# An hgrn2, LRU and attention stack on one core: y transposed right behind its gates, and the even layer's gate products in other PSUM banks

## The chip, the cores and the metric

The program runs on one core of one Trainium2 chip. A core has a matrix engine (PE; its weight loads are listed apart as PEld), a vector engine (DVE), a scalar engine (ACT), a general engine (POOL), and a queue engine (SP) that here issues most of the DMAs. The metric is the device time of one execution in microseconds (us), the median over several executions.

## The reference

The input is 256 tokens of width 1024, in fp32. Two first layers run, then an even layer, a feed-forward block, an odd layer and another feed-forward block. Cut to what the change touches:

```python
# first layer, half of the mix: a gated recurrence
o  = hgrn2_chunkwise(q, log_f, k, v)      # S_t = diag(f_t) S_{t-1} + k_t v_t^T ; o_t = S_t^T q_t
y1 = rmsnorm(o, onorm) * silu(hz) * sigmoid(hgo)
# first layer, other half: compressed, selected and window attention
y2 = (g0 * o_cmp + g1 * o_slc + g2 * o_win) * silu(nz)
h  = h + concat(y1, y2) @ wout            # K = 8 tiles of 128: y1 is tiles 0 to 3, y2 is 4 to 7
h  = h + gate(rmsnorm(h) @ wpg) * (p @ wpp)
# even layer: a short convolution (tiles 0 to 3) beside a linear recurrence (tiles 4 to 7)
lru  = scan(a_t, i_t)                     # a, i from block-diagonal gates
y    = concat(short_conv(...), lru * gelu(x @ ga))
h    = h + y @ eout
```

## The kernel before

The 256 tokens are two halves H = 0 and 1 of 128 rows. A weight comes in as `raw` tiles of 128x1024 by DMA from SP (3 buffers); ACT rounds it to `whi`, DVE forms the rest `wlo<-raw,whi` (5 buffers each). Each fp32 product is three fp32r matmuls at L365: whi with the high part of the input, wlo with the high part, whi with the low part. So one K tile of 512 columns is a triple of matmuls. A tile framework orders the instructions of each engine by a plan made when the program is built, from the order in which the code names them, the dependences and the free buffers; on the chip each engine then goes through its list in order, and waits where an operand or a buffer isn't ready.

The products go to PSUM banks in five pools: `acc` (3 banks), `pA` (2), `pM`, `pB` and `pC` (1 each). `pacc(name)` takes the next bank of `acc`, `ps_(name, "pA")` the next of `pA`. A bank is taken again when the last reader of its former tile has ended.

In a first layer, `nsa(H, ...)` is a generator of the attention of half H: `as` (scores on PE), `anm` (maxima, DVE), `pr` (exponentials on ACT with a row sum, then scaled by `af` on DVE), `apt` (pr transposed, PE L1056), `pts` (copied by DVE), `no` (times v, PE). Its steps are spread over the list between the projections, so that the products of `hz` and `hgo` (the gates of the recurrence's output `y`), `nz` (four groups of 24 matmuls of 256 columns, two groups to a bank of `acc`) and `pp` (24 matmuls of 512 columns) stand between a score group and the transposes that need its exponentials. `to_x(y, H, ys[H], ...)` transposes the gated rows `ys[H]` by four PE transposes at L406 into one bank of `acc` (`xT`), which ACT (`yA<-xT,colp`, L263) and DVE (`yA<-xT,colp,yA`, L409) turn into the high and low parts of the K tiles 0 to 3 of `yA`. `out_proj` then multiplies `yA` by `wout` in two column halves, into tiles `po` of `acc`; `h` takes them, is transposed (`xT<-ident,h`, L431), and `pg` follows.

In the even layer, `gates(j)` puts the block-diagonal gates (`lg`) in `pA`; `short(j)` makes tiles `cpv` (in `acc`), `cc` and `bp`; `gate(j)` makes `ga` (24 matmuls of 256 columns), and DVE's `lga<-ga,R` is the only reader of that bank. `out_proj` follows with `po` in `acc`.

Of the kernel before, what the change touches and what calls it, by code (L numbers as in the profile page):

```python
# [19 lines left out]
T = 256  # L20
# [203 lines left out]
def body(ctx: ExitStack, tc: tile.TileContext, a: dict, offs: dict, out: bass.AP):  # L224
# [14 lines left out]
    def s1(name, dt=F32, tag="s1"):  # L239
        return wk.tile([P, 256], dt, tag=tag, name=name, bufs=BUFS[tag])  # L240

    def s2(name, dt=F32, tag="t2"):
        return wk.tile([P, 512], dt, tag=tag, name=name, bufs=BUFS[tag])
# [7 lines left out]
    def ps_(name, tag):  # L251
        return pp.tile([P, 512], F32, tag=tag, name=name, bufs=BUFS[tag])

    def pacc(name):
        return ps_(name, "acc")

    def dma(o, i):
        nc.sync.dma_start(o, i)
# [3 lines left out]
    def act(o, i, f, **kw):  # L262
        A.activation(o, i, f, **kw)  # L263

    def tt(o, x, y, op):
        V.tensor_tensor(o, x, y, op=op)  # L266
# [65 lines left out]
    def cp(name, j=0, n=1):  # L332
        o = offs["col"][name] + j
        return colp[:, o:o + n]
# [16 lines left out]
    def wgroup(mat, tab, name, then=None, home=None):  # L351

        off, nk, n = offs[tab][name]
        per = min(nk, max(1, 1024 // n))
        res = []
        for k in range(0, nk, per):
            c = min(per, nk - k)
            (hi, lo), = wload(mat, off + k * n, c * n, home)
            res += [(hi[:, j * n:(j + 1) * n], lo[:, j * n:(j + 1) * n]) for j in range(c)]
            if then is not None:  # L360
                then(k)
        return res
# [13 lines left out]
    def proj_both(x, w, name, tag="acc", mid={}, late=False):  # L376

        ps = [ps_(f"{name}{H}", tag) for H in range(2)]
        n = len(w)
        for kh in range(2):  # L380
            ks = range(kh * n // 2, (kh + 1) * n // 2)
            ids = [(k, H) for H in range(2) for k in ks] if kh and late else [(k, H) for k in ks for H in range(2)]
            for k, H in ids:
                if H == 0 and k in mid:
                    mid[k]()
                mm3(ps[H][:, :w[k][0].shape[1]], xk(x, k, H), w[k], k == 0, k == n - 1)
        return ps

    def proj_fm(o, x, w, ks=range(8)):
        for k in ks:  # L390
            mm3(o, w[k], xk(x, k), k == 0, k == 7)

    def new_x(name):
        t = xp.tile([P, 8, 2, T], F32R, tag="x", name=name)
        return t[:, :, 0], t[:, :, 1], t
# [5 lines left out]
    def to_x(x, H, src, gain):  # L401

        sl = slice(H * P, (H + 1) * P)
        ps = ps_("xT", "acc")
        for j in range(4):
            PE.transpose(ps[:, j * P:(j + 1) * P], src[:, j * P:(j + 1) * P], ident)  # L406
        p3 = ps.rearrange("p (k t) -> p k t", k=4)
        act(x[0][:, :4, sl], p3, AF.Identity, scale=gain)
        V.scalar_tensor_tensor(x[1][:, :4, sl], p3, gain, x[0][:, :4, sl], op0=OP.mult, op1=OP.subtract)  # L409
# [179 lines left out]
    def first_layer(l, nx, nxt, whf=None, lb=None, between=None, whq=None, then=lambda: None):  # L589
# [59 lines left out]
        for j in range(0, 4, 2):  # L649
            ps = pacc("hq")  # L650
# [24 lines left out]
        for H in range(2):  # L675
            ps = pj[H]
# [14 lines left out]
        for H in range(2):  # L691
            ps = pj[H]
# [22 lines left out]
        ys = [s2("y", tag="y") for H in range(2)]  # L715
# [17 lines left out]
        for H in range(2):  # L733
            ps = pq[H]
# [27 lines left out]
        for H in range(2):  # L762
            ps = pj[H]
# [10 lines left out]
        y = new_x("yA")  # L774
# [4 lines left out]
        for nm in ("hz", "hgo"):  # L779
            w = win(nm)  # L780
            pj = proj_both(x, w, nm)
            for H in range(2):
                t = s2("gate", tag="gate")
                act(t, pj[H], AF.Tanh, scale=rs[H][1])
                if nm == "hgo":
                    V.scalar_tensor_tensor(t, t, 1.0, gt[H], op0=OP.add, op1=OP.mult)
                    V.scalar_tensor_tensor(ys[H], t, rs[H][0], ys[H], op0=OP.mult, op1=OP.mult)
                else:
                    V.scalar_tensor_tensor(t, t, 1.0, pj[H], op0=OP.add, op1=OP.mult)
                    gt.append(t)  # L790
        zs = []
        for j in range(0, 4, 2):
            ps = pacc("nz")
# [15 lines left out]
        for c, nm in enumerate(("a", "b")):  # L809
            w = wgroup(f"wpp{l}", "pp", nm)  # L810
            pj = proj_both(px, w, "pp")
            for H in range(2):
                ps = pj[H]
                t = s2("pw", tag="lf")
                act(t, ps, AF.Copy, scale=0.5)
                pw[H, c] = t
        for H in range(2):
            to_x(y, H, ys[H], cp("onorm", l))
        for H in range(2):
            sl = slice(H * P, (H + 1) * P)  # L820
            t = s2("yn", tag="t2").rearrange("p (j t) -> p j t", j=4)
# [267 lines left out]
    def even_layer(nx, nxt):  # L1089
        x = nx.x  # L1090
        win = lambda nm: wgroup("ein", "ein", nm)
        y = new_x("yC")
        pa = [ps_("xa", t)[:, :T] for t in ("pB", "pC", "acc", "acc")]
        wa = [win(f"xa{j}") for j in range(3)]
        for j in range(3):
            proj_fm(pa[j], x, wa[j], range(4))
            if j != 1:
                nx.turn(j // 2)
        for j in range(3):
            proj_fm(pa[j], x, wa[j], range(4, 8))  # L1100
        proj_fm(pa[3], x, win("xa3"))
        R = nx.rows()
        R2 = s1("R2", tag="R")
        tt(R2, R, R, OP.mult)
        bd = wk.tile([P, 1024], F32, tag="w8", name="bd", bufs=BUFS["w8"]).rearrange("p (a b c) -> p a b c", a=2, b=4)
        dma(bd.rearrange("p a b c -> p (a b c)"), a["bd"])
        lr, lt = (s4(n).rearrange("p (j t) -> p j t", j=4) for n in ("lr", "lt"))
        li = s4("li").rearrange("p (j t) -> p j t", j=4)

        xcs = []  # L1110

        def conv(j):
            xr = s1("xr", tag="lf")
            tt(xr, pa[j], R, OP.mult)
            xc = s1("xc", tag="gate")
            act(xc, xr, AF.Identity, scale=cp("lcw3", j), bias=cp("lcb", j))
            for k in range(1, 4):
                conv_sh(xc, xr, cp(f"lcw{3 - k}", j), k)
            xcs.append(xc)

        def gates(j):
            xc = xcs[j]
            pg = ps_("lg", "pA")
            for n in range(2):
                mm(pg[:, n * T:(n + 1) * T], bd[:, n, j, :], xc)
            act(lr[:, j, :], pg[:, :T], AF.Tanh, scale=0.5, bias=lp["ba"][:, j:j + 1])
            act(li[:, j, :], pg[:, T:], AF.Tanh, scale=0.5, bias=lp["bx"][:, j:j + 1])

            z, z2 = lp["sp"][:, j:j + 1], lp["sp2"][:, j:j + 1]
            act(lt[:, j, :], lr[:, j, :], AF.Tanh, scale=z, bias=z)  # L1130
            act(lr[:, j, :], lr[:, j, :], AF.Exp, scale=z2, bias=z2)
            V.scalar_tensor_tensor(li[:, j, :], li[:, j, :], 1.0, xc, op0=OP.add, op1=OP.mult)
            V.scalar_tensor_tensor(li[:, j, :], lr[:, j, :], 1.0, li[:, j, :], op0=OP.add, op1=OP.mult)

        def scan():
            act(lt, lt, AF.Sqrt, scale=0.25)
            tt(li, li, lt, OP.mult)
            for n in range(4):
                V.tensor_tensor_scan(lt[:, n, :], lr[:, n, :], li[:, n, :], 0.0, op0=OP.mult, op1=OP.add)

        def gate(j):
            ps = pacc("ga")[:, :T]
            proj_fm(ps, x, win(f"ga{j}"))
            g = s1("lga", tag="t2")
            tt(g, ps, R, OP.mult)
            act(g, g, AF.Gelu_apprx_tanh)
            tt(g, g, lt[:, j, :], OP.mult)
            split(y, 4 + j, slice(0, T), g)

        def short_in(j):  # L1150
            pc = pacc("cpv")
            proj_fm(pc[:, :T], x, win(f"cp{j}"))
            proj_fm(pc[:, T:], x, win(f"vb{j}"))
            return pc

        def short(j, pc):
            c = s1("cp", tag="pr")
            tt(c, pc[:, :T], R2, OP.mult)
            tt(c, pc[:, T:], c, OP.mult)
            o = s1("cc", tag="t2")  # L1160
            act(o, c, AF.Identity, scale=cp("scw2", j), bias=cp("scb", j))
            conv_sh(o, c, cp("scw1", j), 1)
            conv_sh(o, c, cp("scw0", j), 2)
            tt(o, o, R, OP.mult)
            pb = ps_("bp", ("pM", "pB", "pC", "pM")[j])[:, :T]
            proj_fm(pb, x, win(f"bp{j}"))
            tt(o, pb, o, OP.mult)
            split(y, j, slice(0, T), o)

        for j in range(4):  # L1170
            conv(j)
        pc = short_in(0)
        for j in range(4):
            gates(j)
        for j in range(4):
            if j == 2:
                scan()
            short(j, pc if j == 0 else short_in(j))
        for j in range(4):
            gate(j)  # L1180
        nx = nxt()
        out_proj("eout", y, nx.part)
        return nx
# [296 lines left out]
```

## Time and profile before

| | before |
|---|---|
| median of 3 executions | 1014.35 us (1013.6 to 1016.02) |
| profiled execution | 1014.08 us, of which the span is 1012.3 us and 1.8 us lie around it |
| PE busy | 982.1 us, 97% of the span |
| PEld, DVE, ACT busy | 841.3, 824.9 and 624.0 us |
| TensorE clock granted | 0.997 in the mean |

The span is the time from the first to the last instruction that the profiler recorded. PE's busy time is modelled: a matmul's record is longer than its step in the pipeline, so records overlap, and a short gap can vanish in them. In a timeline of PE the distance from one start to the next is the true pace. An idle time in square brackets stands ahead of the instruction that waited, with what ended the wait.

### The profile page before, as it was taken

Reading aid. Unit: us, or ns where it says so; the run is one execution under the profiler, and the core shown is the slowest. Engines: PE = TensorE matmul, PEld = TensorE weight load, DVE = VectorE, ACT = ScalarE, POOL = GpSimd, SP = SyncE. Lnnn points to the kernel's source line nnn. Section 1 sums busy time; section 2 is a strip of 40 time slices with the busy share of each in tenths; the row PEclk is TensorE's granted clock in tenths of the full one; section 3 lists DMA queues with packets and bytes.
Section 4 is the critical chain, followed back from the end, with each engine's and each line's share of the span. In section 5 each row is a group of like instructions: output and inputs, shape, how many; then the busy total and the mean of one; then the engine's idle time right before and its main releaser. Section 6 shows DMA issues by size and latency. Waiting matters only on the chain.

```text
span 1012.3 us, 16208 instructions
## 1 busy us (share of the span) xinstructions
PE 982.1 (97%) x6009; PEld 841.3 (83%) x6009; DVE 824.9 (81%) x1482; ACT 624.0 (62%) x1128; POOL 45.7 (5%) x52
## 2 busy tenths in 40 slices
PE   9999999999998999999999999999999999999997
PEld 6889786788797876799889888888898889888885
DVE  5878899878788898779879988888677889888886
ACT  7753565577644664666657666666756457666664
POOL 1001100000002000000111000000000020000000
PEclk9999999999999999999999999999999999999999
DMA  8832533664504526555754766666572546766661
GB/s 320 304 104 74 181 114 109 215 194 137 182 11 129 164 63 184 170 158 165 231 185 132 223 195 189 191 192 181 167 226 66 169 127 198 215 187 188 187 188 62
DMA packets 49103, 169.02 MB, mean 167 GB/s; under 512 B 5760, under 2 KB 7040, under 8 KB 48384
## 3 DMA queue, kind: packets, MB, share of 16 engines
q1 hardware_dynamic: 48448, 167.17, 54.1%
q8 instruction: 47, 0.77, 0.3%
q10 hardware_dynamic: 576, 0.82, 0.2%
q14 instruction: 32, 0.26, 0.1%
HBM read 165.34 MB, written 1.05 MB: 164 GB/s over the span
## 4 chain that ended last, share of the span: by engine, by line
PE 64%; DVE 9%; ACT 4%; DMA 4%; issue 2%; POOL 1%; POOLq 0%; ACTq 0%; DVEq 0%; SPq 0%
PE up L365 25%; PE pd L365 11%; PE po L365 5%; PE pg L365 3%; DVE wlo L266 3%; PE oq L365 2%; ACT whi L263 2%; PE as L365 1%; PE xT L431 1%; PE xa L365 1%; PE pl L365 1%; PE nz L365 1%; PE hgo L365 1%; PE og L365 1%; PE Q L365 1%
## 5 line engine op out<-in xcount | busy, mean ns | idle before, releaser
L266 DVE TENSOR_TENSOR wlo<-raw,whi 128x1024 fp32r<-128x1024 f32 (+2 forms) x297 | 358.6, 1211 | 86.7 <-ACT whi L263 86.1
L263 ACT ACTIVATE whi<-raw 128x1024 fp32r<-128x1024 f32 (+2 forms) x297 | 309.6, 1045 | 164.8 <-DMA raw<-in_win_dram 17.8
L365 PE MATMUL up<-xN,whi 128*128 128x512 f32 x512 | 180.8, 397 | 0.0
L365 PE MATMUL up<-xN,wlo 128*128 128x256 f32 x512 | 133.3, 281 | 0.0
L365 PE MATMUL pd<-whi,fhl 128*128 128x512 f32 x352 | 115.4, 391 | 0.1
L365 PEld LDWEIGHTS up<-xN,whi 128*128 128x128 f32 x512 | 94.1, 188 | 18.6
L365 PEld LDWEIGHTS up<-xN,wlo 128*128 128x128 f32 x512 | 96.6, 189 | 5.7
L1073 DVE SCALAR_TENSOR_TENSOR fc<-fp,colp,fc 128x255 f32<-128x255 f32 (+1 forms) x176 | 81.5, 479 | 3.0 <-ACT fc L263 0.7
L365 PEld LDWEIGHTS pd<-whi,fhl 128*128 128x128 f32 x352 | 66.0, 188 | 13.0 <-ACT fhl L263 0.5
L365 PE MATMUL pd<-wlo,fhl 128*128 128x512 f32 x176 | 68.6, 390 | 0.0
L263 ACT ACTIVATE upl<-up 128x256 f32<-128x256 f32 x64 | 24.5, 383 | 59.4 <-PE up L365 59.3
L263 ACT ACTIVATE fc<-fp,colp 128x256 f32<-128x256 f32 x88 | 51.0, 590 | 3.9 <-DVE fp L266 3.8
L365 PE MATMUL po<-whi,yA 128*128 128x512 f32 x128 | 41.5, 399 | 2.4 <-ACT yA L263 1.3
L263 ACT ACTIVATE pr<-as,anm 128x128 f32<-128x128 f32 (+1 forms) x80 | 32.5, 422 | 17.8 <-PE apt L1056 6.8
L365 PE MATMUL pg<-whi,xB 128*128 128x512 f32 x128 | 40.6, 393 | 0.0
L365 PEld LDWEIGHTS pd<-wlo,fhl 128*128 128x128 f32 x176 | 33.1, 188 | 6.9
L365 PE MATMUL up<-xD,whi 128*128 128x256 f32 x192 | 35.2, 284 | 0.9 <-DVE xD L436 0.6
L365 PE MATMUL up<-xF,whi 128*128 128x256 f32 x192 | 35.2, 284 | 0.9 <-DVE xF L436 0.6
L266 DVE TENSOR_TENSOR fp<-up,upl 128x256 f32<-128x256 f32 x64 | 27.0, 421 | 10.7 <-ACT upl L263 10.5
L365 PE MATMUL K<-whi,xA 128*128 128x280 f32 (+1 forms) x128 | 33.8, 345 | 0.0
L263 ACT ACTIVATE jk<-h 128x512 f32<-128x512 f32 x36 | 22.7, 637 | 17.4 <-DVE h L266 17.4
L412 POOL TENSOR_TENSOR r<-v,mh 128x2 f32<-128x2 f32 (+1 forms) x10 | 6.7, 672 | 582.0 <-DVE v L472 196.5
(397 smaller groups left out, 2272.6 us busy)
## 6 DMA issues: line engine op xcount, KB each, us to landing
raw<-in_up_dram SPq DMA_DIRECT2D x88, 512.0 KB, 3.6
raw<-in_win_dram SPq DMA_DIRECT2D x62, 512.0 KB, 4.3
raw<-in_down_dram SPq DMA_DIRECT2D x44, 512.0 KB, 3.7
raw<-in_ein_dram SPq DMA_DIRECT2D x20, 512.0 KB, 4.0
raw<-in_oin_dram SPq DMA_DIRECT2D x20, 512.0 KB, 3.8
raw<-in_wout_dram SPq DMA_DIRECT2D x16, 512.0 KB, 3.7
raw<-in_wpg_dram SPq DMA_DIRECT2D x16, 512.0 KB, 4.0
cw<-in_cw_dram SPq DMA_DIRECT2D x4, 1024.0 KB, 7.8
```

The lines of the kernel that those rows point to most:

```text
L263: A.activation(o, i, f, **kw)
L266: V.tensor_tensor(o, x, y, op=op)
L365: PE.matmul(o, l, r, start=start, stop=stop)
L412: G.tensor_tensor(o, v, mh[:, :v.shape[1]], op=OP.pow)
L431: PE.transpose(ps[:, j * P:(j + 1) * P], hc[:, j * P:(j + 1) * P], ident)
L1073: V.scalar_tensor_tensor(dst[:, k:], src[:, :T - k], w, dst[:, k:], op0=OP.mult, op1=OP.add)
```

## The change

In `first_layer` the two `to_x` calls move from behind the `nz` and `pp` products to right behind the two gates. In `even_layer` the four `ga` tiles go to the two banks of `pA` and no longer to the three of `acc`. No arithmetic is added or removed.

```diff
@@ first_layer
                 else:
                     V.scalar_tensor_tensor(t, t, 1.0, pj[H], op0=OP.add, op1=OP.mult)
                     gt.append(t)
+        for H in range(2):
+            to_x(y, H, ys[H], cp("onorm", l))
         zs = []
         for j in range(0, 4, 2):
             ps = pacc("nz")
...
                 act(t, ps, AF.Copy, scale=0.5)
                 pw[H, c] = t
-        for H in range(2):
-            to_x(y, H, ys[H], cp("onorm", l))
         for H in range(2):
@@ even_layer
         def gate(j):
-            ps = pacc("ga")[:, :T]
+            ps = ps_("ga", "pA")[:, :T]
             proj_fm(ps, x, win(f"ga{j}"))
```

Both `xT` banks of y are now taken from `acc` ahead of those of `nz`. The first `nz` bank was free early before; now it follows two more tiles in the turn of three banks. In PE's list of the first layer of the program, here the attention of H = 0 (`as` scores, `apt` transposes of the exponentials), rows with - stand only before, with + only in the changed kernel:

```order
 L365 MATMUL as<-causal,identb 128x2x128
-L365 MATMUL nz<-xA_108,wlo 128x256
-L365 MATMUL nz<-xA_108,whi 128x256 x2
-L365 MATMUL nz<-xA_108,wlo 128x256
-L365 MATMUL nz<-xA_108,whi 128x256 x2
-L365 MATMUL nz<-xA_108,wlo 128x256
 L365 MATMUL as<-kA,qs 128x512 x2
 L365 LDWEIGHTS identb
 L365 MATMUL as<-causal,identb 128x2x128
+L406 MATMUL xT<-ident,y 128x128 x4
+L1056 MATMUL apt<-ident,pr 128x128 x4
+L406 MATMUL xT<-ident,y 128x128 x4
```

The `nz` products between the score groups have left this place, and y's transposes stand behind the last score group; the `nz` products now come behind them. From there back to the first `as` group of row 132.79 and on to the `apt` group of row 143.81 (rows 3, below) the list had 39 of them, and has 4; in the second layer, to the same `apt` group, it had 51 and has 1.

Later in the same list, where the attention of H = 1 ends and `out_proj` begins (`pts` are the transposed exponentials, `po` the output products):

```order
+L1056 MATMUL apt<-ident,pr 128x128 x4
 L365 MATMUL no<-ces,VB 128x512
 L365 MATMUL no<-pts_1367,vv 64x256 x8
-L1056 MATMUL apt<-ident,pr 128x128 x8
-L406 MATMUL xT<-ident,y 128x128 x8
-L365 MATMUL po_1939<-whi,yA 128x512
-L365 MATMUL po_1939<-wlo,yA 128x512
```

Before, y's eight transposes stood right ahead of the first `po`; they are gone from here, and `apt` groups of H = 1 that had `po` between them now have `nz` and `pp`.

In SP's list of the second layer (`sgub` are two small constant tiles of the next layers, whose buffer the transposed y releases; `bd` are the block-diagonal weights):

```order
-L258 DMA raw<-in_wout_dram 128x1024 x4
+L258 DMA raw<-in_wout_dram 128x1024
 L258 DMA sgub<-in_sgub_dram 64x4x128 x2
-L258 DMA raw<-in_wout_dram 128x1024
+L258 DMA raw<-in_wout_dram 128x1024 x5
 L258 DMA bd<-in_bd_dram 128x1024
-L258 DMA raw<-in_wout_dram 128x1024 x3
+L258 DMA raw<-in_wout_dram 128x1024 x2
```

The two `sgub` loads stand three weight tiles earlier. In the even layer no engine's list is changed; only the bank that each `ga` tile takes, and so what it waits for, is another: with two banks the third `ga` tile takes the bank of the first, and must wait for its `lga<-ga,R`.

## Rows read from the trace of the kernel before

**Rows 1.** The page: busy time of each engine, and one group (mean in ns).

```profile
PE 982.1 (97%) x6009; PEld 841.3 (83%) x6009; DVE 824.9 (81%) x1482; ACT 624.0 (62%) x1128; POOL 45.7 (5%) x52
...
L266 DVE TENSOR_TENSOR wlo<-raw,whi 128x1024 fp32r<-128x1024 f32 (+2 forms) x297 | 358.6, 1211 | 86.7 <-ACT whi L263 86.1
```

**Rows 2.** Windows: stretch, its length, busy PE, PEld, DVE, ACT, POOL, clock, DMA.

```profile
132.80:143.80 11.00, 10.97 (x80) 9.49 (x80) 10.44 (x26) 7.40 (x28) 0.08 (x2) 1.00 0.20 55
143.80:197.00 53.20, 51.76 (x293) 39.44 (x292) 49.83 (x92) 30.34 (x69) 0.18 (x3) 1.00 0.45 149
345.00:358.00 13.00, 13.00 (x92) 11.07 (x91) 12.37 (x28) 9.04 (x35) 0.00 (x0) 1.00 0.25 67
358.00:401.00 43.00, 40.66 (x237) 30.01 (x237) 36.32 (x73) 21.77 (x52) 0.00 (x0) 1.00 0.39 118
```

**Rows 3.** Timeline of PE, first layer, attention of H = 0: start, us, operation.

```profile
132.79 0.74 PE L365 MATMUL as<-kA,qs 128*128 128x256 f32 x4
...
139.62 0.63 PE L365 MATMUL as<-kA,qs 128*128 128x512 f32 x2
...
142.62 1.03 PE L365 MATMUL cs<-kcT,qnT 128*128 128x32 f32 x8
...
143.81 0.60 PE L1056 MATMUL apt<-ident,pr 128*128 128x128 f32 x4
```

**Rows 4.** Timeline of ACT and of DVE in the same stretch.

```profile
139.20 0.24 ACT L263 ACTIVATION_READ_ACCUMULATOR pr<-as,anm 128x1 f32 x1
...
140.82 0.74 DVE L787 SCALAR_TENSOR_TENSOR y<-gate,r,y 128x512 f32<-128x512 f32 x1
```

**Rows 5.** Timeline of PE, first layer, y's transposes and the first output product.

```profile
168.34 1.04 PE L406 MATMUL xT<-ident,y 128*128 128x128 f32 x8
170.71 0.50 PE L365 MATMUL po<-whi,yA 128*128 128x512 f32 x1 [1.34 <-ACT yA L263]
```

**Rows 6.** Timeline of PE and of DVE, second layer, attention of H = 0.

```profile
346.02 0.74 PE L365 MATMUL as<-kA,qs 128*128 128x256 f32 x4
...
358.67 0.49 PE L1056 MATMUL apt<-ident,pr 128*128 128x128 f32 x3
...
354.47 0.72 DVE L787 SCALAR_TENSOR_TENSOR y<-gate,r,y 128x512 f32<-128x512 f32 x1
```

**Rows 7.** Timeline of PE, second layer, waits around the output product.

```profile
379.65 0.63 PE L1056 MATMUL apt<-ident,pr 128*128 128x128 f32 x4 [0.24 <-DVE af L1050]
381.79 0.73 PE L365 MATMUL po<-whi,yA 128*128 128x512 f32 x2 [1.04 <-DVE yA L409]
400.70 1.25 PE L431 MATMUL xT<-ident,h 128*128 128x128 f32 x8 [1.04 <-DVE h L266]
```

**Rows 8.** Second layer: SP's timeline, and its longest wait on PE.

```profile
379.00 1.41 SPq L258 DMA_DIRECT2D sgub<-in_sgub_dram  x2
...
SPq L258 <- PE xT L406: 13.7, 1, 13.7
```

**Rows 9.** Even layer, timeline of PE: third gate tile's start, and the output product.

```profile
493.11 0.40 PE L365 MATMUL ga<-xC,whi 128*128 128x256 f32 x2
...
498.87 0.40 PE L365 MATMUL po<-whi,yC 128*128 128x512 f32 x1
...
499.34 0.39 PE L365 MATMUL po<-whi,yC 128*128 128x512 f32 x1
501.19 0.50 PE L365 MATMUL po<-whi,yC 128*128 128x512 f32 x1 [1.47 <-DVE lga L266]
```

**Rows 10.** Even layer, timeline of DVE: the first two readers of the gate banks.

```profile
494.90 0.41 DVE L266 TENSOR_TENSOR lga<-ga,R 128x256 f32<-128x256 f32 x1
...
497.59 0.42 DVE L266 TENSOR_TENSOR lga<-ga,R 128x256 f32<-128x256 f32 x1
```

**Rows 11.** First layer, DVE's reciprocal, and PE's first wlo of the second column half.

```profile
183.27 3.35 DVE L1416 RECIPROCAL lbm<-lbm 128x512 f32<-128x512 f32 x1
...
188.50 0.39 PE L365 MATMUL po<-wlo,yA 128*128 128x512 f32 x1
```

## The prediction

> **What bounds the kernel now.** I read the page first. PE is busy for 97% of the span, DVE for 81%, ACT for 62% [rows 1]. No work is added or removed, so the time can change only by PE's idle time: the question is where PE waits, and what other work it has there.
>
> I then cut the first layers into windows [rows 2]. In the attention of H = 0 (132.8 to 143.8 us in the first layer, 345 to 358 in the second) PE has no gap at all, at a granted clock of 1.00. From there to `pg` it idles by the records for 53.20 - 51.76 = 1.4 us in the first layer and 43.00 - 40.66 = 2.3 us in the second. A 512-column record is 0.39 us long, but the next starts 0.23 us later, so each gap hides another 0.16 us: with some 6 gaps 2.4 us in the first layer, with some 10 about 3.9 us in the second. PE's timeline gives the gaps their names: `po` waits 1.34 us for ACT's `yA`, the high part of y's transposes that stand right ahead of it [rows 5]; in the second layer `apt` waits 0.24, `po` 1.04 for DVE's `yA`, and the transposes of `h` 1.04 [rows 7]. In the even layer `po` starts at 498.87, and its fourth matmul waits until 501.19 for `lga`, the reader of the gate bank that it takes [rows 9].
>
> **The change part by part.** *y's transposes, attention of H = 0.* The eight transposes cost the same wherever they stand: 1.04 us less a tail of 0.16 is 0.88, or 0.11 each [rows 5]. What moves is the `nz` products, 256 columns wide, as are the `ga` products, of which two groups of 24 ran from 493.11 to 498.87 [rows 9]: 0.12 us each. They are what hides the chain of ACT and DVE in H = 0. The last exponential of a score group ended at 139.44, and the score group that takes its buffer started at 139.62; the second half of y was ready at 140.82 + 0.74 = 141.56 [rows 3, 4]. Neither depends on `nz`, and PE's list now has a transpose of that y ahead of the rest. After it follow four transposes (0.44), four `nz` (0.48) and a group of compressed scores (1.03 less a tail of 0.16, and 0.1 for the mask ahead of it), so this `apt` comes at about 143.45 where it came at 143.81 [rows 3]. From 132.79 the old list needed 11.02 us of PE; the new one needs 11.02 - 35 x 0.12 + 0.9 = 7.7 us in a stretch of 10.66. So **PE idles for 3.0 us**; added up wait by wait along the new list I get 3.4. I take 3.2.
>
> The second layer is the same: 12.65 us from 346.02 to 358.67 [rows 6], less 50 x 0.12, plus 0.9, is 7.55. Its second y ends at 354.47 + 0.72 = 355.19 [rows 6]; with transposes and compressed scores behind it the `apt` comes at about 356.8, 10.8 us after the start. That leaves 3.25 us of idle, and 4.0 wait by wait. I take 3.7.
>
> These waits aren't lost if the moved products fill the gaps of later. *First layer, later:* the wait ahead of `po` goes, since yA has long been there, and most of the small gaps with it: -2.4 (1.9 if the small ones stay). The new list has its own handovers there; the cheapest row for one is the 0.24 us of [rows 7], and I put 0.1 for all (up to 0.9). Net 3.2 - 2.4 + 0.1 = **+0.9 us** (0.2 to 2.4).
>
> *Second layer, later:* the same wait of `po` and the one of `apt` go. The transposes of `h` wait because DVE's `h` stands behind `wlo` of late output weights; SP had waited 13.7 us for y's transposes, with `sgub` at the head of its queue, and issued it only at 379.00, with six output weights behind it [rows 8]. With y transposed some 20 us earlier `sgub` no longer holds SP. I take 3.9 us as gone, and 0.2 for new handovers (up to 0.9). If the `h` wait stays (DVE forms those `wlo` late anyway), 1.04 + 0.16 less is gained. Net 3.7 - 3.9 + 0.2 = **0.0 us** (-0.7 to +2.2).
>
> *The gate banks.* With two banks the third `ga` tile waits for the first `lga`, which ended at 494.90 + 0.41 = 495.31; before, the tile started at 493.11 [rows 9, 10]. From an end on DVE to PE's start 0.05 us pass, so it starts at 495.36, 2.25 us later. The third and the fourth tile lasted 2.88 us each, so the fourth starts at 498.24, just behind the second `lga` (497.59 + 0.42 = 498.01), and `po` at 501.12. It then needs no bank of a gate, and its fourth matmul is there 3 x 0.23 = 0.7 us later, at 501.82 where it was 501.19. So the 1.6 us wait of `po` is not removed but traded for an earlier and longer one: **+0.6 us** (0.3 to 0.9, by what else DVE has ahead of its first `lga`). What is queued behind the waiting tile is the fourth tile and all of `po`; nothing off PE waits for it, since DVE's later `lga` are later still.
>
> The Trainium skill, "Perfetto Trace Analysis", section Optimizing Tensor Performance, Matmuls, says that independent groups of matmuls should rotate through different PSUM banks, so that emptying one overlaps the next group. That speaks against three banks becoming two: by the rule alone a third tile waits here, and the trace has the price, the 2.25 us above against the 1.6 it replaces.
>
> *Sum*: 0.9 + 0.0 + 0.6 = +1.5 us on the profiled execution's 1014.08 (span 1012.3 and 1.8 around it), so **1015.6 us**, 1.2 above the median of 1014.35. About 0.2%, or 2.0 us, is what a measurement of this kernel can tell from no change; the forecast is just inside.
>
> **The rivals.**
> *Faster: the chain of H = 0 shrinks when the fill goes.* I let ACT's and DVE's steps keep most of their old times. But some exponentials started when PE's `as` came, and that came behind `nz`. If the early idle time is half of what I take, 1.6 and 1.85 us go, and the time is 1015.6 - 3.4 = 1012.2. For it: the score groups of H = 0 do come earlier. Against: the group at 139.62 stood only 0.18 us behind its release [rows 3, 4], so there the chain already set the pace. Chance 0.2.
>
> *Slower: the fill of H = 1 is thinner.* Between a score group and the transposes of its exponentials H = 1 had `pp` matmuls at 0.23 us; now many of these places have `nz` at 0.12. Some 10 such places in each layer; if each lets PE wait 0.15 us (less than the 0.24 of the `apt` in [rows 7]), it is 20 x 0.15 = 3.0 us, 1018.6. It makes the kernel measurably slower from 0.04 us a place. For it: the same exchange makes the waits of H = 0. Against: H = 1 now has more matmuls in all, and `pp` still stands in its second part. Chance 0.23.
>
> *Slower: the reciprocal.* In the first layer DVE's list now has the reciprocal of 3.35 us ahead of the `wlo` that the second column half of `po` needs first. It ended at 183.27 + 3.35 = 186.62; with 1.21 for a `wlo` the weight is there at 187.83, and PE wanted it at 188.50 [rows 1, 11]. Slack 0.67 us: if DVE is 3 us late there, 2.3 us are lost, 1017.9. Chance 0.06.
>
> *Slower: the clock.* PE's idle time now comes as a dozen short waits in 10 us, twice. Before, with waits up to 1.47 us, the granted clock was 1.00 in every stretch of [rows 2]. If it fell from 2.4 to 1.2 GHz behind such waits, the paces of 0.12 and 0.23 us would double; some 5 us of matmuls at the lower level in each layer cost 10 us, 1025. The Trainium skill, "TensorE: Matmul & The Clock Gate", section A second HAM failure mode, tells of such a fall where PE idles briefly and often between groups. No stretch of this trace shows it. Chance 0.04.
>
> *Nothing comes of it.* The lists differ, so this needs the idle times to cancel: 1014.1 to 1014.4. It is inside the forecast's own range.
>
> **How the numbers follow.** The forecast with its bounds (1013.3 to 1017.5) has 0.47, faster 0.2, thin fill 0.23, reciprocal 0.06, clock 0.04. The range from 1012.0 to 1018.8 takes in the two large rivals at their likeliest and leaves out their far ends and the clock. Below 1012.3 is faster by over 0.2%, above 1016.4 slower: the faster rival and little else give 0.2; of the forecast a sixth lies above 1016.4 (0.08), with thin fill from its lower end on, reciprocal and clock that makes 0.35; the rest, 0.45, is no change that can be told.
>
> **What would show it.** In the profile after, PE should wait ahead of `as`, `apt` and y's `xT` in H = 0, 3 to 4 us in each first layer (windows at 133 to 144 and 346 to 358 with that much less busy PE), and the waits of `po` on `yA` should be gone. SP should no longer wait for `xT` at L406 for 13.7 us. In the even layer a `ga` matmul should wait about 2.2 us for `lga`, and `po` none. The forecast is wrong if the early waits are under 2 us a layer, if `po` still waits for weights or for `h`, or if H = 1 has waits of its own of over 1 us a layer.

## The result, and the profile after

The changed kernel took 1021.47 us (median of 4, 1019.9 to 1022.27) beside 1015.06 us of the kernel before (median of 4): a ratio of 1.0061, with a 95% interval of 1.0041 to 1.0082. It is slower by some 6 us. 1015.6 us had been forecast, with a range of 1012.0 to 1018.8; the time lies above the range. The profiled execution is one of 1022.27 us, 8.2 us above that of before (1014.08).

The page of the changed kernel, its span and its busy times, which answer to [rows 1]:

```profile
span 1020.5 us, 16215 instructions
PE 986.1 (97%) x6009; PEld 845.7 (83%) x6009; DVE 826.6 (81%) x1482; ACT 624.6 (61%) x1128; POOL 46.3 (5%) x52
```

The same work fills 8 us more, and PE's busy time has grown by 4 us. Longer busy time for the same matmuls already points to something beside waits: matmuls that take longer.

To find the place I compared starts: the same instruction in both traces, and the distance from one to the next. From the first score group of H = 0 (132.79 in [rows 3]) to the next part's first product `F` the first layer took 88.63 us and takes 92.38; from the score group at 346.02 [rows 6] to the even layer's first product `xa` the second layer took 89.98 and takes 91.08; from the first `ga` to the first `up` the even layer took 36.61 and takes 39.35. That is +3.75, +1.1 and +2.7, 7.6 of the 8.2 us; the rest came ahead of the change and in the odd layer.

PE's timeline in the first layer, attention of H = 0, answers to [rows 3]:

```profile
134.73 0.74 PE L365 MATMUL as<-kA,qs 128*128 128x256 f32 x4 [0.29 <-ACT pr L263]
137.16 0.66 PE L1056 MATMUL apt<-ident,pr 128*128 128x128 f32 x4 [0.16 <-DVE pr L266]
138.65 0.73 PE L365 MATMUL as<-kA,qs 128*128 128x512 f32 x2 [0.83 <-ACT pr L263]
140.04 1.22 PE L365 MATMUL as<-kA,qs 128*128 128x512 f32 x2 [0.54 <-ACT pr L263]
141.30 1.06 PE L406 MATMUL xT<-ident,y 128*128 128x128 f32 x4
145.23 0.60 PE L1056 MATMUL apt<-ident,pr 128*128 128x128 f32 x4
```

Four waits, 0.29 + 0.16 + 0.83 + 0.54 by the records, each with another 0.16 behind a record's tail: 2.5 us. But look at the durations too. The score group at 140.04 lasts 1.22 us, the equal one at 138.65 lasts 0.73; four transposes last 1.06 where four of the same kind (the `apt` at 145.23) last 0.60. The windows of 1 us say why (the columns are those of [rows 2]; the granted clock is the third figure from the end):

```profile
139.00:140.00 1.00, 0.50 (x3) 0.10 (x1) 0.72 (x3) 0.99 (x6) 0.00 (x0) 1.00 0.00 0
140.00:141.00 1.00, 0.95 (x2) 0.50 (x2) 0.98 (x3) 0.00 (x0) 0.00 (x0) 0.51 0.00 0
141.00:142.00 1.00, 1.00 (x6) 0.94 (x6) 1.00 (x3) 0.00 (x0) 0.00 (x0) 0.50 0.00 0
142.00:143.00 1.00, 1.00 (x6) 1.00 (x5) 0.12 (x1) 0.60 (x1) 0.00 (x0) 0.50 0.00 0
143.00:144.00 1.00, 1.00 (x8) 0.96 (x8) 0.75 (x2) 0.22 (x2) 0.00 (x0) 0.78 0.00 0
```

Right behind the waits the clock fell from 1.00 to 0.50, from 2.4 to 1.2 GHz, and came back in the window of 143. Summed over these windows 0.49 + 0.50 + 0.50 + 0.22 = 1.7 us of full speed were lost. The `apt` that came at 143.81 comes at 145.23.

The second layer has the same waits and no fall of the clock:

```profile
351.21 0.73 PE L365 MATMUL as<-kA,qs 128*128 128x256 f32 x4 [0.32 <-ACT pr L263]
355.37 0.73 PE L365 MATMUL as<-kA,qs 128*128 128x512 f32 x2 [1.65 <-ACT pr L263]
358.01 0.63 PE L1056 MATMUL apt<-ident,pr 128*128 128x128 f32 x4 [0.93 <-DVE pr L266]
```

With tails, and two smaller ones, 3.9 us. The waits of [rows 5] and of `po` and `apt` in [rows 7] are gone, and so is SP's wait for y's transposes, which answers to [rows 8]; `wlo` holds SP's queue instead:

```profile
SPq L258 <- DVE wlo L266: 51.3, 14, 15.5
SPq L258 <- PE xT L406: 0.9, 1, 0.9
```

In the even layer, PE's timeline around the third gate tile and the first output product (to [rows 9]), then windows of 2 us, then DVE's first reader of a gate bank (to [rows 10]):

```profile
497.90 0.28 PE L365 MATMUL ga<-xC,wlo 128*128 128x256 f32 x1
501.55 0.52 PE L365 MATMUL ga<-xC,whi 128*128 128x256 f32 x2 [3.37 <-ACT yC L263]
501.87 0.41 PE L365 MATMUL ga<-xC,wlo 128*128 128x256 f32 x1
...
505.28 0.40 PE L365 MATMUL ga<-xC,whi 128*128 128x256 f32 x2
...
508.86 0.40 PE L365 MATMUL po<-whi,yC 128*128 128x512 f32 x1
```

```profile
501.00:503.00 2.00, 1.45 (x8) 1.48 (x9) 1.90 (x5) 1.97 (x4) 0.00 (x0) 0.71 0.80 215
503.00:505.00 2.00, 2.00 (x11) 2.00 (x11) 1.50 (x3) 1.82 (x4) 0.00 (x0) 0.50 0.71 184
505.00:507.00 2.00, 2.00 (x18) 2.00 (x17) 1.56 (x4) 0.94 (x1) 0.00 (x0) 0.94 0.65 162
```

```profile
500.99 0.41 DVE L266 TENSOR_TENSOR lga<-ga,R 128x256 f32<-128x256 f32 x1
```

The third tile waits, as forecast, for `lga<-ga,R`, which ends at 500.99 + 0.41 = 501.40. The view puts the wait down to ACT's `yC`, which ends 0.13 us later; but the tile starts 0.15 us behind the end of `lga` in the profile of the gate banks alone too (experiment 1), where `yC` comes only after it. `po` has no wait left. The wait is 3.5 us by pace and not 2.3, and behind it the clock is at 0.50 again.

### The profile page after: what moved, and what is told of

It reads as the page before. It is cut to its first block, busy times and chain, and to the rows that moved or that the text cites. A ratio compares the mean times of both kernels' runs of the same rounds, so it can differ in the third digit from the quotient of the medians.

```text
span 1020.5 us, 16215 instructions
## 1 busy us (share of the span) xinstructions
PE 986.1 (97%) x6009; PEld 845.7 (83%) x6009; DVE 826.6 (81%) x1482; ACT 624.6 (61%) x1128; POOL 46.3 (5%) x52
## 4 chain that ended last, share of the span: by engine, by line
PE 71%; DVE 12%; ACT 6%; DMA 5%; issue 3%; POOL 2%; POOLq 0%; ACTq 0%; SPq 0%; DVEq 0%
PE up L365 24%; PE pd L365 11%; PE po L365 5%; DVE wlo L266 4%; PE pg L365 3%; PE pl L365 2%; ACT whi L263 2%; PE nz L365 2%; PE Q L365 2%; PE as L365 2%; POOL hr L412 2%; DMA raw<-in_win_dram 2%; PE oq L365 2%; PE hz L365 1%; PE hgo L365 1%
```

## The experiments

**A kernel's time hangs on the clock of the run.** Each run has a time and a mean granted clock, and inside one kernel they go together (a correlation of -0.74 over 87 runs). Least squares over the runs of the first five kernels that were compared and of the one before, with one slope for all, give 1.0 us for each 0.001 of mean clock. So the table has beside the ratio the mean clock, and the mean time brought with that slope to a clock of 0.998; there the kernel before stands at 1013.9 to 1014.2 us in three samples of 20 to 35 runs (mean clock 0.9972 to 0.9978). In the profiles the mean clock counts the falls that stand ahead of the program's end: 0.998 or 0.999 in the five profiles with none, 0.996 or 0.997 in the four with one, 0.994 or 0.995 in the three with two, and 0.993 in that of the changed kernel above, which has three: at 140 us, at 501 us and at 761 us in the odd layer.

| kernel | runs | median us | ratio to before, 95% | mean clock | us at 0.998 |
|---|---|---|---|---|---|
| the change | 4 | 1021.47 | 1.0061 (1.0041 to 1.0082) | 0.9942 | 1017.5 |
| the change, again | 6 | 1020.50 | 1.0063 (1.0041 to 1.0085) | 0.9950 | 1018.0 |
| y's transposes only | 12 | 1018.44 | 1.0040 (1.0024 to 1.0055) | 0.9970 | 1018.0 |
| gate banks only | 12 | 1016.59 | 1.0018 (1.0003 to 1.0033) | 0.9956 | 1014.4 |
| y between the nz pairs | 12 | 1013.61 | 0.9987 (0.9973 to 1.0001) | 0.9976 | 1012.9 |
| the same, again | 12 | 1013.35 | 0.9986 (0.9971 to 1.0001) | 0.9976 | 1013.1 |
| gates half acc, half pA | 12 | 1015.07 | 1.0006 (0.9987 to 1.0025) | 0.9963 | 1013.9 |
| y only, gaps filled | 10 | 1018.71 | 1.0043 (1.0030 to 1.0057) | 0.9974 | 1017.9 |
| gate banks only, gap filled | 12 | 1016.85 | 1.0032 (1.0017 to 1.0048) | 0.9962 | 1015.7 |
| gates in one bank | 7 | 1018.96 | 1.0045 (1.0027 to 1.0064) | 0.9944 | 1015.5 |
| y between, gates mixed | 12 | 1015.41 | 1.0012 (0.9997 to 1.0028) | 0.9959 | 1013.4 |
| the change, gaps filled | 9 | 1020.81 | 1.0053 (1.0035 to 1.0071) | 0.9972 | 1019.3 |

**1. Each part alone.** First y's transposes alone:

```diff
-            ps = ps_("ga", "pA")[:, :T]
+            ps = pacc("ga")[:, :T]
```

> Only y's transposes are moved; the gate products stay in the three banks. Theory A (the fill of H = 0 is lost, and at one place the clock falls behind the waits): first layer +3.7 us up to the next layer's first product, second layer +1.1, so +4.8 us over the kernel before. Theory B (the prediction's terms were right and the rest of the 6.4 us came with the gate banks): +0.9 and 0.0, so about +1 us. The waits of H = 0 should read 2.5 us in the first layer and 3.9 in the second, and a granted clock under 1.00 only in the first.

1018.44 us, 1.0040: about +4 us, nearer to theory A's +4.8 than to theory B's +1. But the fall that theory A counted isn't in this profile, and the mean clock, 0.9970, is hardly under that of the kernel before. With no fall in H = 0 the price of the waits can be read by itself: with tails 2.8 us in the first layer (one wait of 0.19 more than above) and 3.9 in the second. PE's timeline, H = 0 and then `pg` of the first layer, and the window over H = 0:

```profile
138.95 0.73 PE L365 MATMUL as<-kA,qs 128*128 128x512 f32 x2 [0.82 <-ACT pr L263]
140.35 0.73 PE L365 MATMUL as<-kA,qs 128*128 128x512 f32 x2 [0.54 <-ACT pr L263]
...
205.38 0.66 PE L431 MATMUL xT<-ident,h 128*128 128x128 f32 x4 [0.59 <-DVE xB L436]
214.98 1.32 PE L431 MATMUL xT<-ident,h 128*128 128x128 f32 x8 [0.30 <-DVE h L266]
```

```profile
132.80:145.00 12.20, 10.18 (x62) 7.10 (x61) 11.21 (x27) 8.57 (x34) 0.27 (x3) 1.00 0.20 63
```

The first layer, from score group to `F`, takes 91.15 us, +2.5, and the second 90.82, +0.8. Of the 2.5 the last 0.9 come in `pg`, where the transposes of `h` wait longer for `xB` and `h` (0.59 and 0.30; the kernel before waited 0.29 at the first of these places). How far one profile can be trusted, the other kernels say. Where the edit leaves the first two layers alone (the kernel before, and experiments 1, 3, 4 and 5 with gate tiles only), the first layer took 88.4 to 88.7 us and the second 90.0 to 90.9; where it leaves the gate banks alone, the even layer's stage took 35.95 to 37.94. So +2.5 is clear of this scatter and +0.8 is not.

Then the gate banks alone, the kernel before with

```diff
-            ps = pacc("ga")[:, :T]
+            ps = ps_("ga", "pA")[:, :T]
```

> Only the gate products' banks are changed. Theory A: the third gate tile waits and the clock falls behind that wait; +2.7 us as in the profile of the changed kernel, or +1.7 if the later landing of the output weights in that profile was chance (wait 2.3 us and not 3.4). Theory B (gate banks are the larger part): +5 us. The prediction's own term, without the clock: +0.6 us.

1016.59 us, 1.0018, +1.8 us by the ratio, theory A's smaller figure. But its profile has the wait without the fall behind it: one row of PE's timeline, and two windows.

```profile
498.38 0.47 PE L365 MATMUL ga<-xC,whi 128*128 128x256 f32 x2 [2.44 <-DVE lga L266]
```

```profile
497.00:499.00 2.00, 0.62 (x5) 0.65 (x6) 1.34 (x5) 1.23 (x2) 0.00 (x0) 1.00 0.68 193
499.00:501.00 2.00, 2.00 (x19) 2.00 (x19) 1.90 (x4) 1.97 (x4) 0.00 (x0) 1.00 0.47 180
```

The wait is 2.6 us by pace, and the stage from `ga` to `up` took 36.92 us, only +0.3, which one profile can't tell from nothing. At a clock of 0.998 the kernel is level with the one before (1014.4 beside 1014.2); what makes it slower is its mean clock, 0.9956. Where the falls of the other runs stood isn't known. The one of this profile stands at 46 us, in the first layer, where the edit changes nothing (PE's timeline, then a window):

```profile
46.95 0.80 PE L365 MATMUL hi<-whi,xA 128*128 128x512 f32 x1 [1.79 <-DVE kn L266]
```

```profile
47.00:48.00 1.00, 1.00 (x3) 0.81 (x4) 1.00 (x2) 0.00 (x0) 0.00 (x0) 0.50 0.60 238
```

The two parts together account for the change: 2.5 + 0.8 + 0.3 = 3.6 us of stages without falls of the clock, and 1017.5 to 1018.0 beside 1013.9 to 1014.2 at equal clock; the rest of the 6.4 us is the clock.

**2. y's transposes a little later.** If the loss comes from the fill that H = 0 lost, one pair of `nz` groups ahead of y's transposes is enough to give it back:

```diff
             zs.append(z.rearrange("p (j t) -> p j t", j=2))
+            if j == 0:
+                for H in range(2):
+                    to_x(y, H, ys[H], cp("onorm", l))
```

with the two `to_x` calls taken from their old place, gate banks as before.

> y's transposes stand between the first pair of nz groups and the second, so the first nz bank comes ahead of theirs and its 48 matmuls are there for H = 0. Theory A: no wait of over 0.3 us in H = 0, the clock stays at 1.00, and the waits of po on yA are gone too: -1.5 us in the first layer, -1.5 to -2.5 in the second, 3 to 4 us faster than the kernel before. Rival (the early place of the transposes costs by itself, by DVE's and ACT's work for yA in the chain of H = 0, not by the fill): still slower than the kernel before, by 2 us or more.

> y's transposes between the two pairs of nz groups, gate banks as before, a second sample (the first gave -0.13% with an interval that just reached over zero). Theory A (fill kept, waits of po gone, -1.0 and -0.6 us by the profile): 1 to 1.5 us faster than before. Rival (the first sample was lucky): no difference.

1013.61 and 1013.35 us, 0.9987 and 0.9986. In the first profile H = 0 is full again, and the waits of `po` and its neighbours are mostly gone; a wait of 1.50 is new in the second layer, where the list has `no` behind DVE's `yn`. In the second profile that wait is there too, and in the first layer `po` waits again, now for the attention's part of `yA`, which stands on ACT behind a weight that came late (the second row here, of the second profile; the windows are of the first):

```profile
380.77 1.12 PE L365 MATMUL no<-ces,VB 128*128 128x512 f32 x2 [1.50 <-DVE yn L824]
...
181.49 0.50 PE L365 MATMUL po<-whi,yA 128*128 128x512 f32 x1 [1.52 <-ACT yA L263]
```

```profile
132.80:145.00 12.20, 12.18 (x91) 10.70 (x92) 11.41 (x26) 7.28 (x28) 0.27 (x3) 1.00 0.16 49
345.00:360.00 15.00, 15.00 (x111) 12.81 (x112) 13.63 (x32) 10.39 (x33) 0.00 (x0) 1.00 0.25 72
```

So transposes earlier than before are no loss by themselves; their place ahead of all the `nz` banks is. The rival's forecast, 2 us slower, is out. This run alone doesn't tell the lost fill from work for `yA` inside H = 0, since here the transposes come behind nearly all of it. The profile of experiment 1 does (ACT's timeline):

```profile
140.05 0.24 ACT L263 ACTIVATION_READ_ACCUMULATOR pr<-as,anm 128x1 f32 x1
...
141.68 0.69 ACT L263 ACTIVATE yA<-xT,colp 128x512 fp32r<-128x512 f32 x1 [1.38 <-PE xT L406]
```

Against the kernel before, the chain of ACT and DVE in H = 0 stands there 0.85 us later from its start to its last exponential (140.05 here, 139.20 in [rows 4]), and the first work for `yA` comes behind that. So PE waited for a chain that had not slowed; what was gone was the fill. Against the kernel before, each of the two samples just reaches over 1. Taken as independent (half-widths of 0.0014 and 0.0015) they give 0.9986 with some 0.001 either way: about 1.4 us faster, less than the 3 to 4 that were expected. The second layer is 0.6 us shorter in both profiles; the first is 1.0 shorter in one and 0.9 longer in the other, so the stages don't settle where the gain in time sits.

**3. No gate tile waits for a gate tile.** The kernel before with

```diff
-            ps = pacc("ga")[:, :T]
+            ps = (pacc("ga") if j < 2 else ps_("ga", "pA"))[:, :T]
```

> The first two gate tiles stay in acc, the last two go to pA: no gate tile takes the bank of another gate tile, and the two po tiles take acc banks that are read early. Theory A: neither a wait of a gate tile nor the 1.5 us wait of po on lga; 1.5 us faster than the kernel before. Rival (the wait only moves on to the next thing that DVE makes late, yC of the gate tiles): 0 to -0.5 us.

1015.07 us, 1.0006: the rival. Neither `ga` nor `po` waits for `lga` any more, and the stage takes 36.57 us where it took 36.61. The wait has moved on, behind `po`:

```profile
512.29 0.66 PE L431 MATMUL xT<-ident,h 128*128 128x128 f32 x4 [2.13 <-DVE h L266]
```

Before, that transpose waited 0.43. So it looks as if the even layer's end is set by DVE, which must form the `wlo` of the output weights between everything else, and not by a bank. In these three profiles PE's gap of about 2 us stands at `po`, at `ga` or at `h`, and the stage lasts the same within the scatter of experiment 1.

**4. Filling the gaps.** If the clock falls because PE waits, useless matmuls in the gaps should hold it. Their result is read by nothing. In H = 0 of both first layers, with y's transposes moved:

```diff
+        pf = pacc("fill")
+        for i in range(11):
+            mm(pf, identb, bm(causal, 4), i == 0, i == 10)
         for H in range(2):
             to_x(y, H, ys[H], cp("onorm", l))
```

> y's transposes moved as in the change, gate banks as before, and 11 matmuls of no use in each first layer (512 columns, 0.23 us each, their result is read by nothing), which the list puts into the gaps of H = 0. Theory A (the waits are real slack of PE, and they at times bring the clock down): the stages last as long as with the move alone (first layer +2.5 us, second +0.9), and the clock's mean over the runs rises from 0.9970 to 0.9975 or 0.998, so 1017.5 to 1018 us, 0.5 to 1 us less than the move alone. Rival (the clock falls by chance wherever PE waits, H = 0 has no part in it): mean clock 0.997 and 1018.5 to 1019 us as with the move alone, or more if the useless matmuls delay the chain.

1018.71 us and a mean clock of 0.9974. The clock rose by less than its scatter from run to run, and the time is in the rival's range: no decision. In this profile the two waits in `pg` are longer than in that of experiment 1:

```profile
204.32 0.66 PE L431 MATMUL xT<-ident,h 128*128 128x128 f32 x4 [0.91 <-DVE xB L436]
214.43 1.32 PE L431 MATMUL xT<-ident,h 128*128 128x128 f32 x8 [0.98 <-DVE h L266]
```

From the first score group of H = 0 to the first transpose of `h` both profiles take 67.1 us: the useless matmuls fit into the gaps and cost nothing there, so the chain of ACT and DVE sets the time of H = 0, and not PE. The first layer's 91.96 us, 0.8 more than without them, come from the two waits for DVE in `pg`.

Between the second and the third gate tile, with the gate banks alone:

```diff
         def gate(j):
+            if j == 2:
+                pf = pacc("fill")
+                for i in range(11):
+                    mm(pf, identb, bm(causal, 4), i == 0, i == 10)
             ps = ps_("ga", "pA")[:, :T]
```

> Gate banks as in the change, y as before, and 11 useless matmuls of 0.23 us (2.5 us, read by nothing) between the second gate tile and the third, which waited 2.6 us there. Theory A (that wait is what brings the clock down in so many runs): mean clock back from 0.9956 to 0.9975, and with 1.0 us for each 0.001 of the mean clock 1015 us or a little less, 2 us under the gate banks alone. Rival (the clock falls elsewhere): mean clock stays at 0.9956 and the time at 1016.8 us.

1016.85 us, mean clock 0.9962: a miss for theory A, which wanted 0.9975. But the gap wasn't filled either. In the profile the matmuls ran for 2.55 us, and then the tile still waited, since DVE's `lga` came later than in experiment 1:

```profile
495.85 2.55 PE L365 MATMUL fill<-causal,identb 128*128 128x512 bf16 x11
499.59 0.47 PE L365 MATMUL ga<-xC,whi 128*128 128x256 f32 x2 [1.19 <-ACT yC L263]
```

Both fills together in the changed kernel, with 16 matmuls at the gate tiles, beside the changed kernel itself:

> The changed kernel once more, beside the kernel before on the same chip, for a larger sample. Theory A (idle time of PE worth 3.5 us: 2.5 and 0.9 in the first layers, 0.3 in the even layer; and about two more falls of the clock per run at 1.7 us each): mean clock 0.994 to 0.995, about 6 us slower. Rival (the first comparison caught an unlucky few runs): mean clock 0.997 like the kernel before, 3.5 to 4 us slower.

> The changed kernel with useless matmuls in the waits that it made: 11 of 0.23 us in H = 0 of each first layer, 16 between the second and third gate tile; nothing reads them. Theory A: the idle time stays lost, but the clock's falls behind it go: mean clock 0.997, 3.5 to 4.5 us slower than before, some 2 us better than the changed kernel. Rival (the clock does not hang on these waits, or useless matmuls cost what they save): as the changed kernel, 6 us slower.

The changed kernel again: 1020.50 us, 1.0063, mean clock 0.9950, as theory A had it. In this profile the four waits of H = 0 in the first layer are those of the first profile to within 0.01 us, and no fall stands behind them; behind a wait of 2.7 us at the third gate tile one does. With the gaps filled the mean clock is 0.9972, the same as that of the kernel before in this sample. But the time is 1020.81 us: at equal clock 1019.3 beside 1018.0. So filling the gaps gave the clock back, and cost as much as that was worth; the 16 matmuls took 3.6 us at a place where the wait had been 2.7 us, and the even layer's stage took 38.08 us where the gate banks alone had 36.92. On the clock theory A is right, on the time the rival. It is the one experiment in which the waits were taken away and the mean clock followed; which of the waits it was, it doesn't say.

**5. More waits, and where the clock falls.** All gate tiles in one bank:

```diff
-            ps = pacc("ga")[:, :T]
+            ps = ps_("ga", "pC")[:, :T]
```

> All four gate tiles take one and the same bank (pC), y as before: each waits for the reader of the one before it. Theory A (waits of gate tiles bring the clock down): three waits, 4 to 5 us for the second tile, 2 to 3 us for the others, the clock falls in nearly every run (mean 0.993 or less), and the stage lasts 5 to 9 us longer; 1020 to 1024 us. Rival (clock by chance): mean clock 0.996 to 0.9975, 1018 to 1020 us by the waits alone.

1018.96 us, mean clock 0.9944, the lowest but one of all kernels, with every one of the 7 runs at 0.996 or below. That lies between the two forecasts of the clock, and the time in the rival's range, under theory A's, since the list set `po` matmuls between the gate tiles. The longest wait, 3.1 us by pace, is one of `po`, put down to its weight `whi`; behind it the clock falls (PE's timeline and a window):

```profile
495.70 0.49 PE L365 MATMUL po<-whi,yC 128*128 128x512 f32 x1 [2.90 <-ACT whi L263]
```

```profile
497.00:499.00 2.00, 2.00 (x7) 1.67 (x8) 1.55 (x4) 1.63 (x3) 0.00 (x0) 0.58 0.67 156
```

Experiments 2 and 3 in one kernel:

> y's transposes between the two pairs of nz groups, and gate tiles half in acc, half in pA. Theory A (the fill stays in H = 0, waits of po go, no gate tile waits): as the first alone, -1.3 us, and the gate banks worth 0 to -0.3: 1013 us, about 1.5 us under the kernel before. Rival (what the first gains is given back by h, which DVE makes late): no faster than the kernel before.

1015.41 us, 1.0012: no gain, as the rival has it, and by two ways. `h` is late, with a wait of 2.4 us by pace, and behind that one the clock falls too (PE's timeline, then windows). The profiles of both these kernels have a second fall at 46 us, as that of the gate banks alone.

```profile
514.04 0.66 PE L431 MATMUL xT<-ident,h 128*128 128x128 f32 x4 [2.24 <-DVE h L266]
```

```profile
514.00:516.00 2.00, 1.96 (x11) 1.84 (x12) 1.80 (x3) 1.59 (x6) 0.00 (x0) 0.71 0.78 244
516.00:518.00 2.00, 2.00 (x6) 1.61 (x5) 2.00 (x8) 2.00 (x8) 0.30 (x1) 0.50 0.81 211
```

The even layer's largest wait and the mean clock of the runs stand in order over the kernels whose other stages are those of before: 1.6 us and 0.9972 to 0.9978 (before), 2.3 and 0.9963 (gates mixed), 2.6 and 0.9956 (gate banks only), 3.1 and 0.9944 (one bank). Neighbours differ by little more than the error of such a mean, about 0.0005. And the length of a wait doesn't decide alone. In the even layer the clock fell behind the waits of 3.5, 3.1, 2.7 and 2.4 us and not behind those of 2.6 and 2.3. At 46 us, in the same work of every kernel, it fell where the row has a wait of 1.54, 1.79, 1.81 or 1.82 us, and not where it has 1.83 or 1.49, nor at shorter ones.

## Why the prediction was wrong

**What held.** The waits of H = 0 came where and because of what was said: 2.5 us (forecast 3.2) and 3.9 us (3.7). The waits of `po` and SP's wait for y's transposes went. The third gate tile waits for the first `lga`, 2.6 us in the profile of the gate banks alone (2.3) and 3.5 in that of the change, and the stage costs +0.3 us without a fall of the clock (+0.6). None of the signs by which the forecast was to show itself wrong came; what made it wrong was not among them.

**The step that failed most: the clock.** The prediction had it as a rival with a chance of 0.04, because "the granted clock was 1.00 in every stretch of [rows 2]". Those were four stretches of one trace. "No stretch of this trace shows it" was not so: the same trace has a fall in the odd layer, behind two waits of 0.6 us for DMAs (PE's timeline, then windows, of the kernel before):

```profile
751.80 0.30 PE L365 MATMUL as<-oqk 128*128 128x128 f32 x1 [0.46 <-DMA oqk<-oqk]
752.61 0.30 PE L365 MATMUL as<-okb,oqk 128*128 128x128 f32 x1 [0.51 <-DMA okb<-okb]
```

```profile
754.00:756.00 2.00, 2.00 (x7) 1.50 (x6) 1.12 (x2) 0.00 (x0) 0.00 (x0) 0.51 0.62 160
756.00:758.00 2.00, 2.00 (x8) 1.63 (x7) 0.00 (x0) 0.00 (x0) 0.00 (x0) 0.63 0.95 184
```

A mean clock of 0.997 in the table of before was the sign of it. The mechanism was named, but its chance was far too low, its price in one place too high (each fall lost 1.7 us, not 5), and the wait at the gate tiles was left out of it. Over the runs the mean clock went from 0.9975 to 0.9942 and 0.9950, which at 1.0 us for 0.001 is 2.5 to 3.3 us of the 6.4, where the sum had nothing. The Trainium skill, "TensorE: Matmul & The Clock Gate", section A second HAM failure mode, describes such falls where PE idles briefly and often between groups. The trace agrees at 140 us, with 0.50 behind four waits of 0.3 to 1.0 us; the fall at 501 us stood behind a single wait of 3.5 us.

**The second: "and most of the small gaps with it".** In the first layer 2.4 us were to be won back later and 0.1 lost, in the second 3.9 and 0.2. With y's transposes alone the first layer lost 2.5 in all and the second 0.8, where +0.9 and 0.0 were forecast. In that profile the idle time of H = 0 was right by the prediction's own reckoning: from the first score group to the last `apt` PE took 10.84 and 11.12 us for 7.7 and 7.55 of work, so 3.1 and 3.6 us were idle. From there to the first transpose of `h`, by the same paces, 1.5 us came back in the first layer and 3.3 in the second. The waits that had a name in a row make most of that: 1.5 us of `po`, and 0.4 + 1.2 + 1.2 = 2.8 of `apt`, `po` and `h`. So the term of -2.4 measured -1.5, and that of -3.9 measured -3.3: much of the idle time made of window sums and tails was still there in the new list, as gaps of 0.1 to 0.2 us. And `pg`, where the sum stopped, got 0.9 and 0.5 us more, in the first layer as waits for `xB` and `h`.

**The rivals.** The fill of H = 1 isn't thin: no wait over 0.25 us stands there in either layer. No wait for the reciprocal showed. The faster rival is out, since the chain of H = 0 kept its length. In the second layer four output weights stood behind `sgub`, not six; the wait of `h` went all the same. And the bounds of the three terms add up to 1013.9 and 1019.6 us, so the bounds given for the forecast, 1013.3 and 1017.5, don't follow from them.

**What stays open.** Whether each fall comes from the wait ahead of it alone: two waits of over 2 us had none behind them, shorter ones in stretches that no edit touched had one, and filling the gaps brought the mean clock back, but no time. Where the falls of the runs without a profile stood is not on record.

## What to carry to other kernels

Before a step is moved ahead in code that a scheduler orders by banks, ask which work its banks were holding back or letting through: here two early banks of transposes took the turn of the products that had hidden a chain of ACT and DVE, and one pair of product groups ahead of them was all the difference. Count as won later only waits that have a row of their own; gaps made of sums and tails may come back in the new list, as here. And where PE runs at full clock, price a new wait by what may follow it too: go through the whole trace for falls of the clock and for the waits ahead of them, and not only through the stretches that the change touches.

## What the runs showed of the hardware that I had not expected

Runs of one and the same kernel differ by up to 8 us (1011.56 to 1019.79 over 35 runs of the kernel before), and part of that goes with their mean clock, 1.0 us for each 0.001. In the 13 profiles, summed in windows of 1 us, the clock fell 13 times ahead of the program's end, and each fall lost the same, 1.7 us, whatever the wait ahead of it (from twice 0.6 us to 3.5). The same waits of the same kernel, those of the changed one in H = 0 of the first layer, had a fall behind them in one profile and none in the other.
